# Neighbourhood attention: probabilities cut into half-precision parts before they are turned, and turned by DMA transposes

## The chip, the cores and the metric

The kernel runs on one core of a Trainium2 chip. Its time is the device time of one execution in microseconds (us), from the first instruction to the last, as a median over runs. The core has five engines with queues of their own: PE (TensorE, the matrix multiplier), DVE (VectorE), ACT (ScalarE), POOL (GpSimd) and SP (SyncE, which here only issues transfers). Each works through its instructions in a fixed order, and they meet through semaphores. Transfers are issued from a queue and carried by 16 DMA engines.

## The reference, cut to what matters

The program is two layers over 1024 latent tokens (a 16 by 64 grid) and 256 context tokens of width 1024. The change touches only the attention of the second layer. Each of 16 heads (64 wide) has every latent token attend to a window of keys around it and to all 256 context tokens:

```
def row_block(r):
    rs = jnp.clip(r - kh // 2, 0, rows - kh)
    ...
    s_loc = jnp.einsum("bcqhd,bicjhd->bhcqij", q_r, k_b).astype(jnp.float32) * scale + bias[None]
    s_loc = jnp.where(col_ok[:, :, None, :], s_loc, -jnp.inf)
    s_ctx = jnp.einsum("bcqhd,bjhd->bhcqj", q_r, kc).astype(jnp.float32) * scale
    s = jnp.concatenate([s_loc.reshape(B_, H, n_chunk, NA_QCOLS, n_loc), s_ctx], axis=-1)
    p = jax.nn.softmax(s, axis=-1).astype(v.dtype)
    ...
    o = (jnp.einsum("bhcqij,bicjhd->bcqhd", p_loc, v_b)
         + jnp.einsum("bhcqj,bjhd->bcqhd", p[..., n_loc:], vc))
```

## The kernel before

Everything is float32 by contract. Products are made from two parts per operand, a high and a low one, so that a product is three matrix multiplications (high by high, high by low, low by high).

The attention is cut into 64 **items**: 8 pairs of heads, two halves of the grid (8 rows each), two heads, two pairs of column chunks. An item holds two chunks of 128 queries (8 rows by 16 columns). For each chunk there are 384 local keys (12 rows by 32 columns) and 256 context keys, so an item has two local blocks of 128 by 384 probabilities and one context block of 128 by 512 for both chunks. `attn_item` (L1724) is a generator with three **stages**, and `attention` (L1698) steps it:

- **Scores** (stage 0): two bias tiles `g` are loaded (L1733; a DMA of 192 KB each on SP's queue, through the helper at L268; the pool behind `g` has four buffers, so two items' worth), and PE forms the context scores and two local score blocks in PSUM.
- **Softmax and turning** (stage 1): DVE takes the context maximum (L1749), adds bias and takes the local maximum in one instruction per chunk (L1752), and negates it (L1754). ACT writes the exponentials with their sums: the context ones into a tile `t` (L1755), the local ones over the bias tile `g` (L1757). Then each block is turned, since the values' product needs the keys on the partitions: PE transposes it in float32, 128 by 128 at a time, into PSUM (L1764, 3 + 4 + 3 of them per item), ACT casts the result to a float16 high part (L1767), and DVE subtracts that to give the float16 low part (L1768).
- **Weighted values** (stage 2): PE multiplies the turned parts with the float16 value parts (30 small products per item, 64 columns wide), and ACT scales the result by the reciprocal sum into `s` (L1794). After the fourth item of a half, `attn_out` (L1800) turns that on PE, splits it and writes it to DRAM (`d<-tk`, from POOL's queue).

Between the stages `attention` runs a filler, `prep`: the projections of the next pair of heads (`attn_prep`, matmuls into `pq`) and, once these are used up, the first part of the attention's output projection. Step k begins item k's scores one step ahead of its softmax, and its values one step behind its softmax. `attn_prep` also loads the value tiles (`t<-d`, 17 DMAs a pair on SP's queue) and moves halves of the query parts across partitions with DMAs on POOL's queue (`s<-s`).

The Python order is only a proposal: a scheduler with a timeline model sets the order in which each engine gets its instructions, and pools of buffers (`pg` for `g` with 4, `pt` for `t` with 6, `pk` for `tk` with 4, `p2` for `s` with 35) decide where an instruction must wait for a free buffer.

Of the kernel before, what the change touches and what calls it, by code (L numbers as in the profile page):

```python
# [12 lines left out]
F16 = mybir.dt.float16  # L13
# [3 lines left out]
MUL, ADD, SUB, MAX, MIN = ALU.mult, ALU.add, ALU.subtract, ALU.max, ALU.min  # L17

P = 128
# [181 lines left out]
class Builder:  # L201
# [1496 lines left out]
    def attention(self, u, fill):  # L1698
        self.prep = {}
        self.od = [[self.DR([P, LAT]) for _ in range(2)] for _ in range(8)]  # L1700
        self.banks = 6
        n = sum(self.attn_prep(0, u))
        prep = (x for pr in range(1, 9) for x in (self.attn_prep(pr, u) if pr < 8 else fill))
        load = (x for pr in range(8) for x in self.attn_load(pr))
        items, done = [], 0
        ahead = 1
        for k in range(64 + ahead):
            it = next(load, None)
            if it is not None:
                items.append(it)  # L1710
            for stage in range(3):
                i = k - ahead - stage
                if 0 <= i < 64:
                    next(items[i], None)
                while done < (k * 3 + stage + 5) * n / 24:
                    done += next(prep)
        for it in items[-2:]:
            for _ in it:
                pass
        self.banks = 8  # L1720
        for _ in prep:
            pass

    def attn_item(self, head, hd, hf, c0, qs, kk, kc, vt, osb, out):  # L1724

        nc, a = self.nc, self.a
        rlo = 4 * hf
        bias, loc = [], []
        pctx = self.PS()
        for i in (0, 1):  # L1730
            c = c0 + i
            b = self.G(F32, 384)
            self.ld(b, a["bias"][head, hf, c])  # L1733
            bias.append(b)
            q = [t[:, c * P:(c + 1) * P] for t in qs]
            for part in (0, 1):
                self.mm(pctx[:, i * 256:i * 256 + 256], q[part], kc, part == 0, part == 1)
        for i in (0, 1):
            c = c0 + i
            q = [t[:, c * P:(c + 1) * P] for t in qs]  # L1740
            ps = self.PS()
            for part in (0, 1):
                kv = kk.rearrange("p (r w) -> p r w", w=64)[:, rlo:rlo + 12, KSTART[c]:KSTART[c] + 32]
                self.mm(ps[:, :384], q[part], kv, part == 0, part == 1)
            loc.append(ps)
        yield
        st = self.pt.tile([P, 16], F32, tag="st", name=self.nm("st"))
        cm, mx, nm, s1, s2, rv = (st[:, 2 * i:2 * i + 2] for i in range(6))
        nc.vector.tensor_reduce(cm, pctx.rearrange("p (i k) -> p i k", i=2), axis=AX, op=MAX)  # L1749
        pc = self.T()  # L1750
        for i in (0, 1):
            nc.vector.tensor_tensor_reduce(bias[i], loc[i][:, :384], bias[i], 1.0, cm[:, i:i + 1], ADD, MAX,  # L1752
                                           mx[:, i:i + 1])
            nc.vector.tensor_scalar(nm[:, i:i + 1], mx[:, i:i + 1], -1.0, None, op0=MUL)  # L1754
            nc.scalar.activation(pc[:, i * 256:i * 256 + 256], pctx[:, i * 256:i * 256 + 256], AF.Exp,  # L1755
                                 bias=nm[:, i:i + 1], accum_out=s2[:, i:i + 1])
            nc.scalar.activation(bias[i], bias[i], AF.Exp, bias=nm[:, i:i + 1], accum_out=s1[:, i:i + 1])  # L1757
        nc.vector.tensor_tensor(s1, s1, s2, ADD)
        nc.vector.reciprocal(rv, s1)
        pts = [None] * 3  # L1760
        for k, src, n in ((1, bias[0], 3), (0, pc, 4), (2, bias[1], 3)):
            ps = self.PS()
            for j in range(n):
                nc.tensor.transpose(ps[:, j * P:(j + 1) * P], src[:, j * P:(j + 1) * P], self.ident)  # L1764
            t = self.S2(F16, 1024)
            w = n * P
            nc.scalar.copy(t[:, :w], ps[:, :w])  # L1767
            nc.vector.tensor_tensor(t[:, 512:512 + w], ps[:, :w], t[:, :w], SUB)  # L1768
            pts[k] = t
        yield  # L1770
        o = self.PS()
        if hf not in osb:
            osb[hf] = self.S2()
        for i in (0, 1):
            c = c0 + i
            ops = []
            for g in range(3):
                gg = hf + g
                v = vt[c][:, gg * P + hd * 64:gg * P + hd * 64 + 64]
                vl = vt[c][:, 512 + gg * P + hd * 64:512 + gg * P + hd * 64 + 64]  # L1780
                ops.append((pts[1 + i], g, v, vl))
            for j in range(2):
                v = vt[4][:, j * P + hd * 64:j * P + hd * 64 + 64]
                vl = vt[4][:, 256 + j * P + hd * 64:256 + j * P + hd * 64 + 64]
                ops.append((pts[0], 2 * i + j, v, vl))
            oo = o[:, i * 64:(i + 1) * 64]
            for n, (t, j, v, vl) in enumerate(ops):
                ph, pl = t[:, j * P:(j + 1) * P], t[:, 512 + j * P:512 + (j + 1) * P]
                self.mm(oo, ph, v, n == 0, False)
                self.mm(oo, ph, vl, False, False)  # L1790
                self.mm(oo, pl, v, False, n == 4)
        for i in (0, 1):
            c = c0 + i
            nc.scalar.activation(osb[hf][:, c * P + hd * 64:c * P + hd * 64 + 64], o[:, i * 64:(i + 1) * 64],  # L1794
                                 AF.Copy, scale=rv[:, i:i + 1])
        if out is not None:
            self.attn_out(out, hf, osb[hf])
        yield
# [412 lines left out]
```

## Time and profile before

| what | us |
|---|---|
| runs | 3013.22, 3014.71, 3016.25 (median 3014.71) |
| profiled execution, its time | 3012.68 |
| its span, first to last instruction | 3010.8 |
| attention, from the first local maximum (L1752) to the last low part (L1768) | 1812.7 to 2280.3 |
| the same as 64 items | 7.3 each |
| PE busy over the span | 2890.9 (96%) |
| DVE, ACT, POOL busy over the span | 2075.4, 1359.2, 479.1 |

The page gives busy time by engine and by group of instructions, and for the idle time before an instruction what ended it. A group is named by the line that issued it, the engine, the operation and "written tile <- read tiles". Most operations go through helpers, so L283 is any matmul, L268 any DMA from SP, L274 any DMA from POOL, L289 the low part of a split, L287 the high part. A busy PE is not PE at its peak: its spans overlap and include its pipeline, so that one instruction's span can be longer than the time it adds.

### The profile page before, as it was taken

Reading aid. Unit: us, or ns where it says so; the run is one execution under the profiler, and the core shown is the slowest. Engines: PE = TensorE matmul, PEld = TensorE weight load, DVE = VectorE, ACT = ScalarE, POOL = GpSimd, SP = SyncE. Lnnn points to the kernel's source line nnn. Section 1 sums busy time; section 2 is a strip of 40 time slices with the busy share of each in tenths; the row PEclk is TensorE's granted clock in tenths of the full one; section 3 lists DMA queues with packets and bytes.
Section 4 is the critical chain, followed back from the end, with each engine's and each line's share of the span. In section 5 each row is a group of like instructions: output and inputs, shape, how many; then the busy total and the mean of one; then the engine's idle time right before and its main releaser. Section 6 shows DMA issues by size and latency. Waiting matters only on the chain. (4 is left out here: it accounts for less than half of the span.)

```text
span 3010.8 us, 45798 instructions
## 1 busy us (share of the span) xinstructions
PE 2890.9 (96%) x16320; PEld 2414.9 (80%) x16320; DVE 2075.4 (69%) x3988; ACT 1359.2 (45%) x2545; POOL 479.1 (16%) x789
## 2 busy tenths in 40 slices
PE   7899999899999999999999999999899999999997
PEld 2678888888899788788888888878777788888886
DVE  5677786684677777876777437777767886755555
ACT  3453315453455333333455336777665533333432
POOL 2112013352110111212010000110111021202000
PEclk9999999999999999999999999999999999999999
DMA  7764445356555454658884334444555265525663
GB/s 279 249 222 169 166 166 176 113 185 233 187 182 201 175 179 179 215 189 318 313 297 155 126 128 124 125 135 130 169 189 195 95 246 203 189 102 189 221 192 125
DMA packets 263486, 559.30 MB, mean 186 GB/s; under 512 B 33878, under 2 KB 85784, under 8 KB 263258
## 3 DMA queue, kind: packets, MB, share of 16 engines
q1 hardware_dynamic: 204474, 371.79, 37.7%
q0 software_dynamic: 56480, 180.40, 16.7%
q10 hardware_dynamic: 2304, 4.20, 0.4%
q8 instruction: 128, 2.10, 0.3%
q14 instruction: 100, 0.82, 0.1%
HBM read 418.63 MB, written 119.80 MB: 179 GB/s over the span
## 5 line engine op out<-in xcount | busy, mean ns | idle before, releaser
L1283 PE MATMUL ps<-s,s 128*128 128x512 f32 x2028 | 503.6, 390 | 9.2 <-ACT g L1288 3.5
L1283 PEld LDWEIGHTS ps<-s,s 128*128 128x128 f32 x2028 | 379.6, 188 | 93.8 <-ACT g L1288 6.4
L283 PE MATMUL ps<-s,wh 128*128 128x256 f32 (+1 forms) x1780 | 397.1, 328 | 3.1 <-DVE s L720 2.0
L283 PEld LDWEIGHTS ps<-s,wh 128*128 128x128 f32 x1780 | 295.2, 189 | 38.2 <-ACT wh L287 2.5
L283 PE MATMUL pq<-s,wh 128*128 128x512 f32 (+1 forms) x972 | 296.1, 383 | 0.7 <-DVE s L2039 0.7
L287 ACT CAST wh<-ws 128x1024 fp32r<-128x1024 f32 (+1 forms) x139 | 142.4, 1025 | 338.7 <-PE ps L283 160.2
L1454 PE MATMUL ps<-s,s 128*128 128x512 f32 (+1 forms) x1000 | 258.0, 383 | 3.2 <-DVE s L289 3.1
L283 PE MATMUL ps<-s,wl 128*128 128x256 f32 (+1 forms) x890 | 258.7, 327 | 1.0 <-DVE wl L289 1.0
L289 DVE TENSOR_TENSOR wl<-ws,wh 128x1024 fp32r<-128x1024 f32 (+1 forms) x139 | 165.4, 1191 | 136.3 <-ACT wh L287 132.9
L287 ACT CAST s<-s 128x1024 fp32r<-128x1024 f32 (+2 forms) x184 | 168.5, 940 | 185.3 <-DMA s<-d 161.5
L283 PE MATMUL ps<-s,s 128*128 128x64 f16 (+3 forms) x2663 | 217.8, 234 | 25.8 <-DVE st L1752 11.8
L287 ACT CAST s<-t 128x512 fp32r<-128x512 f32 (+2 forms) x250 | 139.7, 579 | 182.7 <-DVE t L1262 77.3
L289 DVE TENSOR_TENSOR s<-s,s 128x1024 fp32r<-128x1024 f32 (+2 forms) x162 | 186.9, 1185 | 49.1 <-ACT s L287 48.7
L1454 PEld LDWEIGHTS ps<-s,s 128*128 128x128 f32 x1000 | 184.5, 188 | 41.4 <-DVE s L289 4.9
L283 PEld LDWEIGHTS pq<-s,wh 128*128 128x128 f32 x972 | 175.6, 190 | 33.8 <-DVE s L1667 1.2
L289 DVE TENSOR_TENSOR s<-t,s 128x512 fp32r<-128x512 f32 (+2 forms) x250 | 165.4, 676 | 50.9 <-ACT s L287 31.7
L1283 PE MATMUL ps<-s,wh 128*128 128x512 f32 x608 | 192.2, 393 | 0.0
L283 PE MATMUL ps<-s,mat 128*128 128x512 f32 x684 | 175.7, 402 | 5.2 <-ACT s L287 4.3
L283 PE MATMUL pq<-s,wl 128*128 128x512 f32 (+1 forms) x486 | 179.3, 379 | 0.0
L283 PEld LDWEIGHTS ps<-s,wl 128*128 128x128 f32 x890 | 164.1, 189 | 18.8 <-DVE wl L289 1.7
L283 PEld LDWEIGHTS ps<-s,mat 128*128 128x128 f32 x684 | 130.0, 192 | 39.9 <-ACT s L287 6.6
L1454 PE MATMUL ps<-s 128*128 128x512 f32 (+1 forms) x500 | 149.1, 385 | 0.0
(382 smaller groups left out, 5622.1 us busy)
## 6 DMA issues: line engine op xcount, KB each, us to landing
s<-d SPq DMA_DIRECT2D x282, 256.0 KB, 3.6
s<-in_down SPq DMA_DIRECT2D x150, 256.0 KB, 4.1
d<-s POOLq DMA_DIRECT2D x137, 256.0 KB, 3.3
d<-tk POOLq DMA_DIRECT2D x98, 256.0 KB, 3.4
s<-in_ada_w POOLq DMA_DIRECT2D x48, 512.0 KB, 4.6
g<-in_bias SPq DMA_DIRECT2D x128, 192.0 KB, 2.8
ws<-in_up SPq DMA_DIRECT2D x44, 512.0 KB, 3.3
d<-g POOLq DMA_DIRECT2D x87, 256.0 KB, 3.2
```

Of the source, the lines that this page charges most:

```text
L283: self.nc.tensor.matmul(o, l, r, start=st, stop=sp)
L287: self.last_hi = nc.scalar.copy(hi, src).ins
L289: self.last_lo = eng.tensor_tensor(lo, src, hi.bitcast(F32), SUB).ins
L1283: nc.tensor.matmul(ps, x[:, sl], y, start=first and j == 0 and x is wh and y is xh, stop=j == 3 and x is wl, skip_group_check=True)
L1454: m = nc.tensor.matmul(acc[j][:, c0:c1], x[:, sl], y[:, xs], start=first and k == 0, stop=last and k == 2, skip_group_check=True)
```

## The change

Each of the three blocks of an item is now cut into its float16 parts where it lies, queries on the partitions: high and low part side by side in one tile `x` of 128 by 2w (w is 384 or 512). ACT casts the two local blocks (into `tk`), DVE casts the context block (into `t`). DVE subtracts for the local blocks, POOL for the context block. Then one DMA transpose per block, on SP's queue, writes the turned parts to the tile that the values' product reads. PE's transposes and the PSUM tiles for them are gone. The biases are loaded from POOL's queue instead of SP's, and the weighted values of an item come a step later than before (two steps behind its softmax); the loop runs one step more.

```
-        for k in range(64 + ahead):
+        for k in range(65 + ahead):
...
-                i = k - ahead - stage
+                i = k - ahead - stage - (stage == 2)
...
-            self.ld(b, a["bias"][head, hf, c])
+            self.ldr(b, a["bias"][head, hf, c])
...
         for k, src, n in ((1, bias[0], 3), (0, pc, 4), (2, bias[1], 3)):
-            ps = self.PS()
-            for j in range(n):
-                nc.tensor.transpose(ps[:, j * P:(j + 1) * P], src[:, j * P:(j + 1) * P], self.ident)
+            w = n * P
+            x = self.T(F16, 1024) if k == 0 else self.TK(F16, 1024)
+            if k:
+                nc.scalar.copy(x[:, :w], src[:, :w])
+            else:
+                nc.vector.tensor_copy(x[:, :w], src[:, :w])
+            (nc.vector if k else nc.gpsimd).tensor_tensor(x[:, w:2 * w], src[:, :w], x[:, :w], SUB)
             t = self.S2(F16, 1024)
-            w = n * P
-            nc.scalar.copy(t[:, :w], ps[:, :w])
-            nc.vector.tensor_tensor(t[:, 512:512 + w], ps[:, :w], t[:, :w], SUB)
-            pts[k] = t
+            nc.sync.dma_start_transpose(t[:, :2 * w].rearrange("p (n c) -> p n c", c=P), x[:, :2 * w])
+            pts[k] = (t, w)
...
-            for n, (t, j, v, vl) in enumerate(ops):
-                ph, pl = t[:, j * P:(j + 1) * P], t[:, 512 + j * P:512 + (j + 1) * P]
+            for n, ((t, w), j, v, vl) in enumerate(ops):
+                ph, pl = t[:, j * P:(j + 1) * P], t[:, w + j * P:w + (j + 1) * P]
```

The scheduler then sets the orders anew. Three places show what moved. Numbers behind a name count tiles, so one name with one number is one tile.

SP's queue, late in the attention. Before, it holds the bias loads of item after item, with a value load among them (`t<-d` reads the values):

```order
L268 DMA t_23077<-d_16236 128x2x128
L268 DMA g_23019<-in_bias 128x384
L268 DMA g_23023<-in_bias 128x384
L268 DMA g_23122<-in_bias 128x384
L268 DMA g_23126<-in_bias 128x384
L268 DMA g_23245<-in_bias 128x384
```

With the change, at a like place (the `s<-d` rows load finished heads for the output projection):

```order
L1770 DMA_TRANSPOSE s_4758_22560<-tk_22557 128x6x128
L1770 DMA_TRANSPOSE s_4760_22565<-t_22562 128x8x128
L1770 DMA_TRANSPOSE s_4762_22570<-tk_22567 128x6x128
L268 DMA t_22680<-d_16236 128x2x128
L268 DMA s_4816_22849<-d_16979 128x512
L268 DMA s_4829_22926<-d_16980 128x512
L268 DMA s_4830_22928<-d_16981 128x512
L268 DMA s_4846_22980<-d_16982 128x512
L1770 DMA_TRANSPOSE s_4778_22665<-tk_22662 128x6x128
L1770 DMA_TRANSPOSE s_4780_22670<-t_22667 128x8x128
```

The biases have left SP, and three transposes an item stand between the loads of values, weights and finished heads, each behind the softmax of its item.

POOL's queue, a stretch within the attention. Before it held only transfers, here the query halves (`s<-s`) and finished heads (`d<-tk`):

```order
L274 DMA s_4499_21381<-s_4499_21381 64x512
L274 DMA s_4500_21382<-s_4500_21382 64x512
L274 DMA d_16984<-tk_21431 128x512
L274 DMA s_4501_21387<-s_4501_21387 64x512
L274 DMA d_16985<-tk_21432 128x512
```

Now:

```order
L274 DMA g_22531<-in_bias 128x384
L274 DMA d_16986<-tk_22506 128x512
L274 DMA d_16987<-tk_22507 128x512
L1768 TENSOR_TENSOR t_22562<-t_22546,t_22562 128x512
L274 DMA g_22629<-in_bias 128x384
L274 DMA g_22633<-in_bias 128x384
L1768 TENSOR_TENSOR t_22667<-t_22651,t_22667 128x512
L274 DMA g_22725<-in_bias 128x384
```

The context block's subtraction (L1768 on POOL) stands between the bias loads of later items, and the bias loads stand between the subtractions, so each can hold up the other.

DVE's queue. Before, the subtractions read PSUM and come right after the cast that precedes them, and the bias tile had been freed by PE:

```order
L1768 TENSOR_TENSOR s_4795_23156<-ps_23152,s_4795_23156 128x384
L1768 TENSOR_TENSOR s_4797_23164<-ps_23159,s_4797_23164 128x512
L1754 TENSOR_SCALAR st_23266<-st_23266 128x1
L1768 TENSOR_TENSOR s_4799_23171<-ps_23167,s_4799_23171 128x384
```

Now the subtraction is what frees a bias tile: `g_22412` and `g_22416` belong to one item, `g_22527` and `g_22531` to the next, and `g_22629`, the first bias of the third, needs one of their four buffers:

```order
L1768 TENSOR_TENSOR tk_22557<-g_22412,tk_22557 128x384
L1754 TENSOR_SCALAR st_22649<-st_22649 128x1
L1759 RECIPROCAL st_22544<-st_22544 128x2
L1768 TENSOR_TENSOR tk_22567<-g_22416,tk_22567 128x384
L1767 CAST t_22667<-t_22651 128x512
L1758 TENSOR_TENSOR st_22649<-st_22649 128x2
L1759 RECIPROCAL st_22649<-st_22649 128x2
L1768 TENSOR_TENSOR tk_22662<-g_22527,tk_22662 128x384
L1648 SCALAR_TENSOR_TENSOR s_4749_22520<-t_22515,c_16968,s_4749_22520 128x512
L1768 TENSOR_TENSOR tk_22672<-g_22531,tk_22672 128x384
L1752 ISA g_22629,st_22742<-ps_22637,g_22629,st_22742 128x384
```

Six rows lie between the subtraction that frees the second tile and the first use of a bias loaded into the pair.

## The prediction

> **What bounds the kernel now.** I read the stage's engine times first, since the change lies inside one stage, under the page's head.
>
> ```profile
> span 3010.8 us, 45798 instructions
> ```
>
> ```profile
> core 0: us, PE busy (x) PEld busy (x) DVE busy (x) ACT busy (x) POOL busy (x), PEclk, DMA share, GB/s
> 1815.00:2285.00 470.00, 438.66 (x4090) 378.59 (x4090) 343.91 (x910) 337.08 (x972) 60.13 (x113) 0.99 0.49 149
> ```
>
> The attention takes 470 us for 64 items, 7.3 us each. PE is busy for 439 of them and idle for 31; DVE and ACT have 126 and 133 us to spare, POOL does little, the DMA engines are used by half, the granted clock is 0.99. So PE sets the pace, but not alone: the waits of the engines in this stretch say more (who waited, for whom; us in total, times, longest).
>
> ```profile
> PE ps L283 <- DVE st L1752: 11.8, 11, 2.7
> PE ps L1764 <- DVE s L1768: 5.3, 9, 0.7
> SPq L268 <- PE ps L1764: 319.9, 111, 8.9
> DVE g L1752 <- DMA g<-in_bias: 5.6, 4, 2.6
> ```
>
> PE waits for DVE to free score banks and transpose banks. The third row is of SP's own queue: 111 times a load stood there until a transpose had freed a bias tile, 320 us in all. So biases are fetched as late as the four tiles allow, though the fourth row shows that DVE paid for it only 4 times. The chain of waits over this stretch has the three dearest cases:
>
> ```profile
> 1996.94 4.44 DMA g<-in_bias
> 2106.08 3.95 DMA g<-in_bias
> 2171.77 6.16 DMA g<-in_bias
> ```
>
> **What the change removes.** All 640 transposes leave PE, the casts of 64 x 3 blocks from PSUM leave ACT, as many subtractions leave DVE.
>
> ```profile
> 1815.00:2285.00 470.00, 88.07 (x640) 73.49 (x640) 0.99 0.49 149
> 2053.39 1.09 PE ps L1764 x10
> L1767 ACT CAST s<-ps 128x384 f16<-128x384 f32 x128 | 61.7, 482 | 36.3 <-PE ps L1764 34.9 <-PE ps L283 0.5
> L1767 ACT CAST s<-ps 128x512 f16<-128x512 f32 x64 | 37.6, 588 | 2.4 <-PE ps L283 2.0 <-PE ps L1764 0.2
> L1768 DVE TENSOR_TENSOR s<-ps,s 128x384 f16<-128x384 f32 x128 | 70.6, 552 | 16.1 <-ACT s L1767 14.3 <-DMA s<-s 1.0
> L1768 DVE TENSOR_TENSOR s<-ps,s 128x512 f16<-128x512 f32 x64 | 43.8, 684 | 8.1 <-ACT s L1767 7.7
> ```
>
> The first row is the transposes alone: 88 us of spans, which overlap. The chain has ten in a row in 1.09 us, and that is the time that they add: 64 x 1.09 = 70 us. Bounds are 70 and 88; I take 70, so PE keeps 439 - 70 = 369 us, 5.8 an item. The 10.9 us that PE idled before transposes go too, if no other wait inherits them; I count on none of it.
>
> ACT loses 2 x 0.482 + 0.588 = 1.55 us an item and DVE 2 x 0.552 + 0.684 = 1.79.
>
> **What it adds on the engines.** The new casts and subtractions read SBUF. The nearest rows:
>
> ```profile
> L287 ACT CAST s<-t 128x512 fp32r<-128x512 f32 x213 | 128.2, 620 | 161.4 <-DVE t L1262 77.3 <-POOL t L837 19.4 <-DMA d<-s 16.0
> L1376 DVE TENSOR_TENSOR g<-tk,g 128x512 f32<-128x512 f32 x65 | 44.8, 690 | 1.3 <-ACT g L1416 0.2
> L289 DVE TENSOR_TENSOR s<-s 128x256 fp32r<-128x256 f32 x22 | 8.5, 419 | 0.3 <-ACT s L287 0.3
> L837 POOL TENSOR_TENSOR t<-t,t 128x512 f32<-128x512 f32 x40 | 53.3, 1348 | 57.0 <-DVE t L836 56.0 <-ACT mat L335 0.4
> L783 POOL TENSOR_TENSOR s<-s,s 128x512 f32<-128x512 f32 x4 | 7.1, 1794 | 0.8 <-PE ps L283 0.8
> L274 POOL DMA_DIRECT2D s<-s x60 | 31.2, 521 | 163.9 <-ACT s L1679 101.6 <-DVE s L1768 16.1 <-ACT s L1794 10.6
> ```
>
> ACT: two casts of 384 columns, between 0.48 (the PSUM row above) and 0.62: 0.5 each, 1.0 an item, half a microsecond less than before. DVE: a 384-column subtraction lies midway between 0.69 and 0.42, 0.55 each; its one copy of 512 columns to half precision has no row; between half of 0.69 and all of it, I take 0.6 since the trace has no DVE copy that is faster. Sum 1.7 an item against 1.79: nothing gained or lost. POOL: one subtraction, 1.35 to 1.79 us, I take 1.35, its 40 instances being nearer in kind; and two bias issues of 0.52. POOL goes from 60 to 60 + 64 x (1.35 + 1.04) = 213 us, by the dearer row 241, of some 420: no bound by its sum.
>
> The Trainium skill (Advanced Engine Details and Errata, GPSIMD Details) says that POOL shares a read and a write interface with DVE and conflicts with DVE instructions that have two SBUF inputs; the new subtractions are such. By that rule DVE could lose POOL's 86 us of subtraction, an estimate: 344 + 86 = 430, some 10 us over the stage that I forecast. No run here shows such a loss.
>
> **The transposes by DMA.** The trace before has none. Each moves 128 x 768 or 128 x 1024 two-byte values, 192 or 256 KB, three an item, 0.66 MB; 41.9 MB in all. Rows for plain transfers of that size, and for SP's queue as a whole, over 1805 to 2285:
>
> ```profile
> q1 hardware_dynamic: 41696, 47.07, 33.3%
> g<-in_bias SPq DMA_DIRECT2D x124, 192.0 KB, 2.8
> s<-s POOLq DMA_DIRECT2D x60, 128.0 KB, 3.4
> d<-tk POOLq DMA_DIRECT2D x30, 256.0 KB, 3.4
> s<-d SPq DMA_DIRECT2D x24, 256.0 KB, 5.5
> ```
>
> Work on the 16 engines: q1 moved 47.07 MB in 33.3% of 480 us, 160 us, so 41.9 MB take 142 us at that rate. With 0.49 x 470 = 230 us of present traffic the sum is 372 us, under PE's 369 plus its idle time, though not by much. Below, nothing could make it cheaper than plain; above, half the plain rate gives 284 and a sum of 514. I take the plain rate, because the only transfer of the trace that also writes SBUF from SBUF (`s<-s`) lands in the same 3.4 us as the others.
>
> Latency: a step is to be some 6.5 us, and values now follow two steps behind the softmax, 13 us. The softmax and the cuts of an item use about 6 of these (five small DVE instructions, four exponentials, two casts, the subtractions); 7 are left for a landing of 2.8 to 5.5. Covered; if the landing were 10, PE, whose queue holds the value products in place, would stand still and everything queued behind them with it, the scores and projections.
>
> SP's queue keeps three instructions an item where two biases were; behind a transpose that waits for its softmax stand value and weight loads, which have an item or more of lead.
>
> **Where the stall goes.** Bias tiles were freed by PE's transposes and are now freed after a cast and a subtraction, and their loads stand in POOL's queue behind a subtraction of 1.35. The loop of one pair of tiles, two items long: landing 2.8, issue 0.52, two bias additions at 0.7, a negation 0.15, the exponentials, two casts 1.0, two subtractions 1.1, POOL's subtraction ahead 1.35. The rows for the remaining links:
>
> ```profile
> L1752 DVE CUSTOM_DVE_ANT_0 g<-ps,g,st 128x384 f32<-128x384 f32 x128 | 75.9, 614 | 46.2 <-PE ps L283 33.7 <-DMA g<-in_bias 5.6 <-DMA s<-d 3.7
> L1757 ACT ACTIVATE g<-g,st 128x384 f32<-128x384 f32 x128 | 79.2, 619 | 0.0
> L1755 ACT ACTIVATE t<-ps,st 128x256 f32<-128x256 f32 x128 | 61.2, 478 | 36.8 <-DVE st L1754 35.0 <-DVE st L1759 1.5
> L1755 ACT ACTIVATION_READ_ACCUMULATOR t<-ps,st 128x1 f32 x128 | 26.2, 204 | 0.0
> L1752 DVE DVE_READ_ACCUMULATOR2_ANT st<- 128x1 f32 x128 | 10.6, 83 | 0.0
> L1754 DVE TENSOR_SCALAR st<-st 128x1 f32<-128x1 f32 x128 | 17.4, 148 | 0.6
> L268 SPq DMA_DIRECT2D g<-in_bias x128: 327/328/1415, 1391.5 to 2269.8; - x128
> ```
>
> Exponentials: 2 x (0.48 + 0.62 + 2 x 0.2) = 3.0. Sum 11.3 us for two items, 5.7 an item; before, with PE's 0.33 for three transposes in place of casts and subtractions and SP's issue of 0.33, it was 8.0, 4.0 an item. So the loop moves from 3 us an item under the pace to just under the new one. Each time one of its links waits behind other work of its engine, a bias comes late. Bounds: nothing, or half of the added 3.3 us on each item, 64 x 1.65 = 106. I take 20 us, nearer the lower end, because DVE paid for late biases only 4 times so far.
>
> At the end the last item's values come one step later with the projection's filler partly used up; I put 4 us for the wait of the last heads, of a step of 6.5.
>
> **Sum.** 3012.68 - 70 + 20 + 4 = 2966.7 on the profiled execution, which lies 2.0 under the median of the runs: **2969 us**.
>
> **Rivals.**
>
> *Late biases eat it all.* The loop above, with waits at five or six of its links of 0.6 us each, comes to 14.6 us per two items, 7.3 an item: today's pace. For it: the 320 us on SP's queue, and POOL's queue, where a bias stands behind subtractions that wait for DVE. Against: only 4 late loads so far. Price: nothing gained or lost but the 4 us of the tail, about 3015, with some 20 us to either side.
>
> *The DMA engines become the bound (the slower side).* If a transposing transfer keeps the engines twice as long as a plain one, they need 514 us for the stage: 514 - 470 = +44, and 4 for the tail, 3063. It decides from 240 / 142 = 1.7 times the plain cost. For it: every value has to reach another partition, which no transfer of the trace does but `s<-s`, and that carries half the bytes in the same 3.4 us. Against: `s<-s` moves whole rows and is the nearest there is, and its landing is no worse than `d<-tk`'s.
>
> *One at a time.* If SP starts a transpose only when the one before has landed, three landings of 3.4 us are 10.2 an item, 653 us for the stage: +183, 3198. For it: one queue issues them all. Against: the bias loads are issued 0.33 us each, without waiting for a landing. The Trainium skill (VectorE: DVE Perf Modes, The three transpose paths) gives 1309 ns for a 128 by 128 block of half precision by DMA against 390 by TensorE; as an estimate, its 20 blocks an item one after another would be 26 us, 1676 for the stage and about 4220 in all. TensorE's blocks cost 109 ns here, so the trace doesn't bear out the other half of that row.
>
> **How the numbers follow.** Forecast 0.56; late biases 0.14 (of it 0.04 faster, 0.05 the same, 0.05 slower); DMA engines 0.20; one at a time 0.10. A measurement can't tell 0.2%, 6 us, from no change. Faster 0.56 + 0.04 = 0.60, the same 0.05, slower 0.05 + 0.20 + 0.10 = 0.35. The forecast's own range: with 88 - 70 = 18 us more from the transposes, the 11 of PE's waits and no late bias, 3014.7 - 88 - 11 + 4 = 2920, of which I use 2930; above, with the 106 us of late biases it ends in the first rival. The range for 8 in 10 reaches over that and the DMA engines' case, 3063 and a dozen more for its tail: **2930 to 3075**, with the one-at-a-time case and a little below left out.
>
> **What would show it.** PE's busy time in the attention near 369 and the stage near 420 us: the removal is right. No row of PE's waits ending in a DMA transpose: the latency is covered; such rows with tens of us mean a rival of the transfers, and the DMA share tells which: near 1 for the engines, below 0.8 for one at a time. DVE's wait for the bias loads near 20 us: the loop is sized right; over 60, the first rival. DVE's subtractions above 0.6 us each would mean contention with POOL. I am wrong if the attention lasts 470 us or longer.

## The result, and the profile after

The changed kernel takes **3088.93 us**, a median of 4 runs (3082.02 to 3094.14), against 3014.46 before (4 runs, 3013.22 to 3016.25): a ratio of 1.0249, 95% interval 1.0235 to 1.0263. It is slower, by 74 us; 2969 was forecast, in a range of 2930 to 3075. The mechanism is that of the rival named after the DMA engines, which was priced at 3063.

| us, in the profiled execution | before | after |
|---|---|---|
| span | 3010.8 | 3080.2 |
| from the start to the first bias addition (L1752) | 1812.7 | 1826.6 |
| first to last bias addition, called the attention from here on | 460.8 | 503.9 |
| from the last one to the end | 737.3 | 749.7 |

So 43 of the 69 us come from the attention, 14 from ahead of it and 12 from behind it. The engines' busy times over the attention in the changed kernel (columns as in the prediction):

```profile
core 0: us, PE busy (x) PEld busy (x) DVE busy (x) ACT busy (x) POOL busy (x), PEclk, DMA share, GB/s
1826.60:2330.50 503.90, 395.59 (x3302) 326.96 (x3301) 353.57 (x899) 305.38 (x889) 198.78 (x289) 0.88 1.04 211
```

PE lost its transposes, 396 us busy and not 430 over the same piece, and now idles for 108 us. The one figure at its limit is the DMA share: 1.04, where 0.48 stood before. (It can pass 1: in the two kernels of transfers below it is up to 1.02 where one queue is at work and 1.04 to 1.14 where two are.) The granted clock has gone from 0.99 to 0.88. What the engines waited for from 1815 to 2365 us, a little over both ends of the attention (who, for whom; us in total, times, longest):

```profile
PE ps L283 <- DMA s<-tk: 56.8, 22, 13.4
PE ps L283 <- DVE st L1752: 23.2, 20, 3.7
PE ps L283 <- DMA s<-t: 14.5, 9, 5.1
ACT tk L1765 <- DMA s<-tk: 60.6, 22, 8.9
DVE tk L1768 <- ACT tk L1765: 51.0, 26, 9.9
DVE g L1752 <- DMA g<-in_bias: 33.4, 26, 4.5
POOL g L274 <- DVE tk L1768: 103.2, 60, 10.8
```

Read from the top, these make one ring. PE waits at the value products for turned blocks, 71 us in all. ACT waits with the next cast because the four tiles `tk` come free only when a transpose has landed. DVE's low parts wait for that cast, POOL's bias loads for the low parts that free a bias tile, DVE's next softmax for the bias. Two of its links end in a transfer, the turned blocks and the biases. The queues' part of the 16 engines in the attention (packets, MB, share of the time), and the median time to landing:

```profile
DMA packets 201270, 106.21 MB, mean 211 GB/s; under 512 B 170572, under 2 KB 186175, under 8 KB 201215
q1 hardware_dynamic: 186911, 60.71, 68.4%
q0 software_dynamic: 14304, 44.84, 34.7%
...
g<-in_bias POOLq DMA_DIRECT2D x124, 192.0 KB, 4.7
...
s<-tk SPq DMA_TRANSPOSE x124, 5.4
...
s<-t SPq DMA_TRANSPOSE x62, 5.8
```

68.4% and 34.7% of 503.9 us are 345 and 175 us, together 520: all the time there is. Some 165 thousand of the packets under 512 bytes are new (5933 stood there before): 40.6 MB of transposes in pieces of about 250 bytes. The chain of waits has the late ones in line (start, us, what):

```profile
2219.15 8.96 DMA s<-tk
...
2230.67 14.18 DMA s<-tk
...
2270.53 9.58 DMA s<-tk
...
2338.05 13.97 DMA s<-tk
```

The last of these lies behind the last softmax: the values of the last items wait for it, and the filler is used up.

### The profile page after: what moved, and what is told of

Its sections match the earlier page's. It is cut to its first block, busy times and chain, and to the rows that moved or that the text cites. A ratio compares the mean times of both kernels' runs of the same rounds, so it can differ in the third digit from the quotient of the medians.

```text
span 3080.2 us, 45180 instructions
## 1 busy us (share of the span) xinstructions
PE 2865.4 (93%) x15680; PEld 2375.8 (77%) x15680; DVE 2093.7 (68%) x3988; ACT 1333.7 (43%) x2481; POOL 628.2 (20%) x981
## 5 line engine op out<-in xcount | busy, mean ns | idle before, releaser
L283 PE MATMUL ps<-s,s 128*128 128x64 f16 (+3 forms) x2663 | 240.7, 241 | 117.9 <-DMA s<-tk 56.8
L283 PE MATMUL pq<-s,wh 128*128 128x512 f32 (+1 forms) x972 | 313.4, 402 | 9.8 <-DVE s L1680 3.6
L283 PEld LDWEIGHTS pq<-s,wh 128*128 128x128 f32 x972 | 189.2, 205 | 44.6 <-DVE s L1680 4.9
L283 PE MATMUL pq<-s,wl 128*128 128x512 f32 (+1 forms) x486 | 187.8, 396 | 0.0
L283 PEld LDWEIGHTS ps<-s,s 128*128 128x128 f32 (+1 forms) x743 | 121.4, 202 | 52.6 <-DVE st L1752 13.9
```

Source lines behind the costliest of these rows:

```text
L283: self.nc.tensor.matmul(o, l, r, start=st, stop=sp)
```

## The experiments

**Is it turning, or moving the bytes at all? The latency, or the rate?** Three kernels vary the transfer alone. The first copies the same bytes and leaves the turning out, the second turns only the high parts and leaves the low ones out, the third gives every transfer a step more.

```
- nc.sync.dma_start_transpose(t[:, :2 * w].rearrange("p (n c) -> p n c", c=P), x[:, :2 * w])
+ nc.sync.dma_start(t[:, :2 * w], x[:, :2 * w])                                         (e1)
+ nc.sync.dma_start_transpose(t[:, :w].rearrange("p (n c) -> p n c", c=P), x[:, :w])    (e6)
- i = k - ahead - stage - (stage == 2)
+ i = k - ahead - stage - 2 * (stage == 2)                                              (e2)
```

> The changed kernel with each DMA transpose replaced by a plain SBUF to SBUF transfer of the same bytes on the same queue with the same waits (the probabilities are not turned, so this leaves the turning out). Theory A, a transposing transfer keeps the 16 DMA engines about twice as long as a plain one and they are full: the DMA share of the attention falls from about 1.05 to 0.9 or less, landings from 5.4 us to under 4, and the time to 2950 to 2990 us. Theory B, late biases through POOL's queue set the pace: the time stays above 3050. Theory C, the bytes themselves are too many whatever the kind: above 3050, with the share still near 1.

> The changed kernel with only the high halves transposed (96 and 128 KB instead of 192 and 256) and the high part used in place of the low one; the low parts are left out of the result. Theory A (DMA engines full by transposes): half of the transposes' time is gone, the share falls to about 0.8, the time to 2960 to 3000 us. Theory B (late biases): above 3050. Theory D, a fixed time per transpose on SP's queue, independent of its size: no gain, SP's row for a transpose stays at 1.26 and 1.52 us and the time above 3050.

> The changed kernel with the weighted values yet another step later. Theory A (full DMA engines, a limit of rate): the time stays at 3070 us or more, since a later consumer does not make the engines faster. Theory E, only the latency of the transposes is uncovered: PE's waits for transposes fall from about 71 us to under 20 and the time to 3020 or less.

Measured, one time each: 3007.7, 3009.25 and 3074.98 us, beside 3014.14 for the kernel before (8 runs, 3008.73 to 3022.69). The attention over its own piece, plain copies first, then half the transposes:

```profile
1832.30:2259.40 427.10, 370.34 (x3343) 309.64 (x3342) 359.85 (x897) 302.78 (x886) 199.05 (x290) 0.94 0.80 248
```

```profile
1822.00:2270.00 448.00, 382.50 (x3360) 319.31 (x3359) 364.12 (x900) 304.58 (x888) 199.95 (x290) 0.92 0.88 192
```

Unturned, the same bytes leave the engines at 0.80 and the attention at 427 us; with half the bytes turned it takes 448, with all of them 504. SP's issue of a transpose took 1.2 us (median) with half the bytes and 1.3 to 1.5 with all, and at 504 us there are 2.7 us for each of the 186 transposes, so it is not SP's issue that fills the stage. With a step more of slack the waits only move:

```profile
PE ps L283 <- DMA s<-tk: 6.8, 2, 5.8
ACT tk L1765 <- DMA s<-tk: 68.1, 23, 12.9
DVE g L1752 <- DMA g<-in_bias: 48.8, 37, 3.2
```

PE's wait for `s<-tk` falls from 57 to 7 us and the attention stays at 499.8. Here slack cured the late transfers, and not the engines that had too much to do. The totals of e1 and e6 are above what was expected: both lose time ahead of the attention (1832 and 1822 against 1812.7), on which more below. So even with the turning left out, the rest of the change was worth about 6 us (3007.7 against 3014.14) and not the 46 that were forecast.

**What a transpose costs by itself.** Two kernels leave out the whole computation. They hold transfers of 256 KB between SBUF tiles, 64 in a stretch with eight tiles to write to, and in some stretches bias loads of 192 KB on GpSimd's queue:

> Leaves out the whole computation (the output is zeros) and runs five stretches of 64 transfers each, one after the other: 256 KB copies from SBUF to SBUF on SP's queue; the same bytes by transposing DMA; 192 KB bias loads on GpSimd's queue; copies and bias loads together; transposes and bias loads together. Theory A (a transposing transfer keeps the 16 engines about twice as long as a plain one, whatever runs beside it): the copies take about 57 us of engine time (16.8 MB at q1's 47.07 MB per 160 us), the transposes 105 to 125 us with the DMA share at 0.9 or more, the bias loads about 43 us, transposes with bias loads about 150 to 170 us, the sum of the two. Rival B (SP's issue of 1.26 us each sets the rate): 64 transposes last 81 us with a share below 0.8, and 85 with the bias loads beside them. Rival C (transposes are only slow beside other traffic): alone 57 to 70 us, with bias loads well over the sum of the two.

> Leaves out the whole computation again (zeros are put out), five stretches of 64 transfers of 256 KB from SBUF to SBUF: copies in rows of 2 KB on SP; copies in pieces of 256 bytes on SP (the tile that is written has gaps); transposes on SP; pieces of 256 bytes with the 192 KB bias loads on GpSimd's queue; transposes with copies on GpSimd's queue. Copies alone ran at 380 GB/s and transposes alone at 190 with the DMA share at 1.0, and transposes with bias loads took 178 us where the two alone add up to about 127. Theory A (the price of a transpose is that of its 256-byte packets): the pieces run at 180 to 200 GB/s too, 85 to 95 us, and beside the bias loads they too take 160 us or more. Rival (the turning itself costs, or SP's issue of 1.3 us): the pieces run at 300 GB/s or more, 55 us or less, and beside the bias loads 100 or less; then the transposes' stretch still takes 88 us.

The stretches of the first in its order (copies; transposes; bias loads; copies with bias loads; transposes with bias loads):

```profile
core 0: us, DVE busy (x) POOL busy (x), PEclk, DMA share, GB/s
15.80:63.50 47.70, 3.61 (x33) 0.00 (x0) 1.00 0.95 352
64.00:152.00 88.00, 2.17 (x19) 0.00 (x0) 1.00 1.00 187
155.00:200.00 45.00, 4.69 (x55) 37.96 (x72) 1.00 0.86 298
203.00:275.00 72.00, 0.82 (x6) 28.32 (x53) 1.00 1.04 380
277.00:455.00 178.00, 3.79 (x37) 34.21 (x64) 1.00 1.08 165
```

And of the second (copies; pieces of 256 bytes; transposes; pieces with bias loads; transposes with copies on GpSimd's queue):

```profile
21.00:64.00 43.00, 2.05 (x19) 0.00 (x0) 1.00 0.99 369
68.00:143.00 75.00, 2.62 (x33) 0.00 (x0) 1.00 1.00 213
149.00:236.00 87.00, 2.30 (x15) 0.00 (x0) 1.00 1.01 188
240.00:347.00 107.00, 2.33 (x28) 34.29 (x64) 1.00 1.08 268
353.00:545.00 192.00, 3.18 (x23) 32.92 (x62) 1.00 1.14 172
```

Alone, with nothing beside it, a transpose keeps the engines 87 / 43 = 2.0 times as long as a copy. Most of that goes with the size of its pieces: a copy in pieces of 256 bytes takes 75 / 43 = 1.7 times (the 75 us lie between the 85 to 95 of the theory and the 55 of its rival). The second half of the theory fell. Beside bias loads on GpSimd's queue the pieces do no harm (107 us, where 75 and 45 add up to 120), nor do whole copies (72, where 43 and 45 add up to 88), but transposes do: 178 us where 88 and 45 add up to 133. Beside copies on GpSimd's queue they took 192, where 87 and 43 (the copies on SP's queue) add up to 130. The 178 hold two parts: up to 384 us the loads and 18 of the transposes are issued, 107 us for what takes some 67 apart (45 for the loads, 22 for the 4.17 MB turned by then), and from 384 the other transposes run alone at their old rate (192 GB/s). So the price is two things: a factor of 2 that transposes show with nothing beside them, and a further one where they meet traffic on GpSimd's queue. Why they slow each other stays open, and no run mixes transposes with a queue other than GpSimd's. In these stretches, copies and transposes had this median time to landing:

```profile
t<-x SPq DMA_DIRECT2D x64, 256.0 KB, 3.0
```

```profile
t<-x SPq DMA_TRANSPOSE x64, 3.4
```

3.0 against 3.4 us, with twice the time on the engines: the landing does not show the price.

**The other two parts of the change, and the kernel before as a control.**

```
- self.ldr(b, a["bias"][head, hf, c])        the changed kernel, biases back on SP (e3)
+ self.ld(b, a["bias"][head, hf, c])
- self.ld(b, a["bias"][head, hf, c])         the kernel before, biases on GpSimd (p1)
+ self.ldr(b, a["bias"][head, hf, c])
- for k in range(64 + ahead):                the kernel before, values an item later (p2)
-     i = k - ahead - stage
+ for k in range(65 + ahead):
+     i = k - ahead - stage - (stage == 2)
```

> The kernel before, unchanged, as a control for what the changed kernels lose outside the attention: in the profile of before GpSimd idles until 16.3 us ahead of its first mask and ScalarE's first square of x starts at 11.97 us; in all five profiles of changed kernels the mask is made at 3.4 us, the square starts at about 16.6, and the attention starts 6 to 20 us later. If that comes from the run and not from the kernel, the square may start at 16.6 here too and the attention at 1817 or later; if it comes from the change, the square starts at 12.0 and the attention's first addition of a bias at 1812.7 within 1.5 us. The attention itself lasts 459 to 463 us in either case, and the time is 3009 to 3023 us.

> The changed kernel with its bias loads back on SP's queue. Theory A (the DMA engines are full): the attention stays at 495 to 510 us and the time at 3075 to 3095, since the same bytes are moved; the DMA share stays over 0.93. Rival (late biases behind GpSimd's subtractions cost their own 20 us or more): the attention falls to 485 or less, the time to 3065 or less. Or the other way: bias loads now stand behind transposes of 1.26 us issue each on SP, which wait for the softmax; then VectorE's wait for biases goes from 33 us to 60 or more and the time above 3100.

> The kernel before with only its bias loads moved to GpSimd's queue. If the queue matters by itself (the prediction's loop), VectorE's wait for biases goes from 5.6 us to 15 or more and the time up by 8 to 20 us. Theory A: biases are late in the changed kernel because the engines that carry them are full; here they are half idle, the wait stays under 10 us, the attention at 461 within 4, the time at 3014 within 6.

> The kernel before with only the values an item later, transposes on PE. Nothing in before waits for the casts (PE waits at the value products for a cast are not among its rows), so the attention stays at 458 to 464 us and the time at 3010 to 3024; the rival that the later values cost by themselves (buffers of turned blocks held longer, the tail) would show as an attention of 466 or more or as 5 us or more after its last bias addition, 737.3 before.

c0: 3012.63 us, with the attention at 1812.7 and 460.6 long, as in the profile of before. (It is one run; p1, as fast as before, begins its attention 6.4 us later.) e3: 3090.25, one time and within the runs of the changed kernel, attention 508.9, DMA share 0.92 (a little under the 0.93 expected). p1: 3012.48 (10 runs, 3003.81 to 3021.15) against 3012.85, a ratio of 0.9990 (0.9975 to 1.0005). p2: 3020.1, one time, attention 467.2 and 739.5 behind it. That is over the 466 at which the later values were to cost something by themselves; 6 us of the attention at most, in a time that the runs of before nearly reach (3008.4 to 3019.45). So the bias queue costs nothing and the later values little beside the 74. DVE's wait for biases in p1 and in e3:

```profile
DVE g L1752 <- DMA g<-in_bias: 9.7, 11, 1.5
```

```profile
DVE g L1752 <- DMA g<-in_bias: 60.1, 33, 10.1
```

On GpSimd's queue with half-idle engines (a share of 0.48) VectorE waits 10 us for biases. Back on SP they stand behind transposes, and SP waits 62 us there for VectorE's low parts: VectorE's wait grows to 60 us, and the total doesn't show it. p1 also gives what the queues cost without the transposes:

```profile
q0 software_dynamic: 14558, 45.69, 32.6%
q1 hardware_dynamic: 21965, 20.41, 14.6%
```

And this is q1 in e1, with the same bytes unturned:

```profile
q1 hardware_dynamic: 48512, 60.18, 42.6%
```

Of 462 us, p1's share is 67 for q1; in the changed kernel it was 345, so the transposes took 277 us, where the same bytes unturned (42.6% of 427.1 us, 182) took 115. Half the bytes turned (e6, q1 at 45.9% of 448 us) took 138, half of 277: it goes by bytes. In the kernel the factor is 2.4: the 2.0 from above, and some 1.2 that fit the mixture. This second factor is no constant: with the biases on SP's queue, and 74 us of GpSimd's traffic in place of 175, the same working gives 242 us, a factor of 2.1 (e3, q1 at 77.4% of 508.9 us, of which 152 are what it carried before).

**Less on the engines.** First only the context block by DMA, the rest as before (e4). Then the same with the local blocks turned a step after their softmax, in a stage of their own (v1), and those stages with no DMA transpose at all (v2):

```
  for stage in range(4):                                        (v1, v2)
      i = k - ahead - stage
  ...
  e = self.TK(F32)                   exponentials beside the bias tile, not over it
  nc.scalar.activation(e[:, :384], bias[i], AF.Exp, ...)
  ...
  nc.sync.dma_start_transpose(t.rearrange("p (n c) -> p n c", c=P), x)     context (v1)
  yield
  ...                                local blocks on PE, as before
```

> Only the context block (256 KB an item) by DMA transpose, the two local blocks by PE as before, biases on SP's queue, values a step later. Theory A: 16.8 MB of transposes are 40% of the added engine time, so the DMA share stays under 0.85 and the landing is covered; PE saves 4 of 10 transposes, 28 us, less some waits: 2985 to 3005 us, a gain on the kernel before. Theory B does not apply (biases are freed by PE as before). Theory D or E: above 3014, with PE waiting for transposes.

> A version after the theory that the DMA engines must not be filled and PE must not wait for the softmax: only the context block is turned by DMA, the two local blocks on PE one step after their softmax (a stage of its own), values a step after that, exponentials of the local blocks written to tiles of their own so that a bias tile comes free at once; biases on SP. Theory A: 16.3 MB of transposes at 190 GB/s are 86 us of engine time on top of 0.48 x 462 = 222, a share near 0.7, so the engines don't bind; PE keeps about 411 us and the waits for ACT's exponentials of the first context-only version (19.7 us) go: attention 430 to 448 us, time 2990 to 3010 with the 5 to 12 us that changed kernels lose before and after it. Rival (ScalarE and VectorE's own loop of softmax and casts sets the pace at 7.2 us an item, whatever PE does): attention 458 or more, time 3015 or more.

> The same stages without any DMA transpose: all ten blocks of an item on PE, one step after the softmax. PE's work is that of the kernel before, 439 us in 470; only its waits of some 20 us can go. Attention 445 to 460 us, time 2998 to 3014. If the softmax loop of ScalarE and VectorE sets the pace, 458 or more and no gain; if the DMA transposes of v1 are worth anything, this is 10 us or more slower than v1.

e4: 3035.71 (5 runs), 1.0065 (1.0044 to 1.0085), 30 us over the top of what was expected. Attention 462.9, DMA share 0.69, transposes landing in 3.3 us: the engines no longer bind, and yet nothing is won, and PE now waits at the local blocks' transposes (L1775 there) for the softmax:

```profile
PE ps L1775 <- ACT g L1757: 19.7, 9, 7.4
```

v1: 3027.19 (4 runs), 1.0052 (1.0037 to 1.0067). Its attention took 446.0, 15 us less than before and as expected; the total wasn't, since 14 us are lost ahead of it and 13 behind. v2: 3021.22 (10 runs), 1.0025 (1.0013 to 1.0038), over the 3014 expected, attention 459.4: the stage by itself brings nothing, and the transposes of v1 are worth 13 us inside the attention. In the total v2 is 6 us shorter than v1, which loses more than that around it.

**What is lost around the attention.** Each of the seven profiles with the context's subtraction on GpSimd starts in another way than the eight without. The timeline of GpSimd and ScalarE in the changed kernel, and in x1, which has that subtraction on VectorE and turns the last two items on PE:

```profile
3.42 0.31 POOL masks.py:199 TENSOR_SCALAR_AFFINE_SELECT c<-c 128x128 f32<-128x128 f32 x1 [0.34 <-issue]
16.59 1.06 ACT L1857 ACTIVATE s<-s 128x1024 f32<-128x1024 f32 x1 [6.12 <-DMA s<-in_x_row]
```

```profile
16.47 0.28 POOL masks.py:199 TENSOR_SCALAR_AFFINE_SELECT c<-c 128x128 f32<-128x128 f32 x1 [13.37 <-issue]
13.18 1.06 ACT L1865 ACTIVATE s<-s 128x1024 f32<-128x1024 f32 x1 [4.31 <-DMA s<-in_x_row]
```

In the first, GpSimd does not stand still for 13 us ahead of its mask; the four large loads queued behind the mask then leave at 3.7 and not at 16.7, beside the rows of x, and ScalarE gets its first row 3.4 us later. That the loads delay the row is argued from this order alone. v3 is v1 with both edits, v4 has the context's cast on ScalarE besides.

```
- (nc.vector if k else nc.gpsimd).tensor_tensor(x[:, w:2 * w], src[:, :w], x[:, :w], SUB)
+ nc.vector.tensor_tensor(x[:, w:2 * w], src[:, :w], x[:, :w], SUB)
+ if head == 15 and hf == 1:         transposes on PE, as before
```

> The changed kernel with the context's subtraction on VectorE instead of GpSimd, and with the last two of the 64 items turned on PE. Theory (the subtraction on GpSimd moves the program's start; the last transposes, which landed in 14 us beside the loads of the next layer, set the tail): ScalarE's first square of x back at 12 to 13 us, first bias addition at 1812 to 1821, and 736 to 742 us behind the last one; the attention itself still 495 to 510, since the engines carry nearly the same bytes; time 3062 to 3078. If neither is the cause: square at 16.4 or later, 748 or more behind, time 3080 or more.

> The version with only the context block by DMA and the local blocks turned on PE in a stage of their own, now with the context's subtraction on VectorE and the last two items turned on PE altogether. The same theory: square at 12 to 13 us, attention from 1812 to 1821, lasting 446 to 455 (VectorE is 43 us busier, 385 of some 450), 736 to 742 behind it: 2996 to 3012 in all, at or under the kernel before. If VectorE has no room: attention 458 or more, 3012 or more.

> v3 with the context's cast to half precision on ScalarE, whose busy time is the lowest of the three: VectorE some 359 us busy, ScalarE some 335. If VectorE's load mattered in v3, the attention is 3 us or more shorter than there; if the chain from softmax to transpose does (ScalarE's cast then stands behind the next exponentials), no shorter. 2994 to 3012 us.

x1: 3057.63 (4 runs, 3055.32 to 3076.91), 1.0152 (1.0116 to 1.0188). First row at 13.18 us, attention from 1819.4 to 2322.7 (503.3, unchanged), 730.9 behind it against 749.7. The start is near what the theory had (12 to 13 us, and 1812 to 1821), the piece behind the attention is shorter than its 736 to 742, and the attention's loss of 43 us stands. Both edits are in x1, so which of them shortened the tail isn't shown. v3: **2999.48** (5 runs, 2994.23 to 3000.36), **0.9942 (0.9925 to 0.9960)**: faster than both kernels.

```profile
1813.20:2246.20 433.00, 401.30 (x3683) 343.54 (x3682) 354.44 (x959) 297.51 (x882) 55.44 (x103) 0.98 0.76 191
```

Attention 433.0, 28 us less than before, though VectorE has more to do than in v1; behind it 746.1 and not the 736 to 742 expected, so there the last transposes were not the cause. v4: 3004.51 (10 runs), 0.9962 (0.9948 to 0.9976), attention 444.4: relieving VectorE was no help. Why v3's attention is 13 us shorter than v1's no run shows; one effect of GpSimd's subtraction on VectorE can be read directly. The groups of the changed kernel in the attention (mean ns behind the bar), and the same subtraction in x1:

```profile
L1768 DVE TENSOR_TENSOR tk<-g,tk 128x384 f16<-128x384 f32 x128 | 86.2, 685 | 51.7 <-ACT tk L1765 51.0
...
L1768 POOL TENSOR_TENSOR t<-t,t 128x512 f16<-128x512 f32 x64 | 76.6, 1198 | 60.8 <-DVE st L1758 21.3 <-DVE st L1754 20.1 <-DVE t L1767 17.8
...
L1765 ACT CAST tk<-g 128x384 f16<-128x384 f32 x128 | 63.4, 511 | 66.5 <-DMA s<-tk 60.6 <-DMA d<-tk 5.1
L1767 DVE CAST t<-t 128x512 f16<-128x512 f32 x64 | 28.4, 444 | 7.8 <-ACT t L1755 6.8 <-issue 0.7
```

```profile
L1776 DVE TENSOR_TENSOR tk<-g,tk 128x384 f16<-128x384 f32 x124 | 67.3, 550 | 45.8 <-ACT tk L1773 45.2
```

VectorE's subtraction takes 685 ns in the mean beside GpSimd's and 550 without; its single instances go up to 1905 ns in the one and to 560 in the other. 128 x 0.135 = 17 us of VectorE's time are lost. The Trainium skill (SBUF — State Buffer, SBUF: two separate sides) has whichever of VectorE, with two inputs in SBUF, and GpSimd starts first hold their shared ports for its whole instruction, while the other waits. The trace agrees as to the waiting: each of the 11 instances over 650 ns that the timeline lists singly overlaps a GpSimd subtraction (median 1173 ns) and ends 0.41 to 0.43 us after it. It doesn't bear out that the first to start goes first: the two longest, 1.91 and 1.81 us, began 0.2 to 0.3 us ahead of GpSimd's and still ended behind it.

## Why the prediction was wrong, step by step

The forecast was off by 120 us: 93 in the attention (50 less forecast, 43 more measured), 14 ahead of it, 8 behind it, and 5 because the profiled execution lies 6.9 us under the median here and 2.0 before.

**What bounds the kernel now: right.** PE set the pace. With the bytes moved unturned (e1) PE is busy for 370 us, 369 forecast, and the attention is 34 us shorter, of the 50 forecast; PE's wait for the softmax (L1752) grew by about the rest, to 31.1 us there against 11.8 before. In the changed kernel itself PE was busy for 396 us, at a granted clock of 0.88: how much of its 43 us went through the lower clock, no run separates.

**The price of the transposes: the step that failed.** The prediction put 41.9 MB at the plain rate, 142 us, "because the only transfer of the trace that also writes SBUF from SBUF (`s<-s`) lands in the same 3.4 us as the others". The plain price was high by a fifth (115 us for 40.6 MB in e1, 138 at that rate). The turned one was 277, not known from any row of before. And the reason given could not have told: in m1 the two kinds land in 3.0 and 3.4 us, while 64 of them take 43 and 87 us of the engines (m2). With 277 in place of 142 and 230 of present traffic the prediction's own sum is 507, against 504 measured; that is no test of its own, since with the engines full the queues' times add up to about the stage whatever it lasts.

**The rival of the DMA engines: right in mechanism and in the stage** (+44 forecast, +43 measured). That the number fits so well is partly luck: its 284 us were 2 x 142, and the measured 277 are 2.4 x 115, so a plain price that was too high made up for a factor that was too low. Twice the 115 and the 230 would have been 460, under the 470 of the stage. Its test, a share near 1 with PE waiting for transposes, is what the page shows. What it lacked is 14 us ahead of the stage and 8 of the 12 behind.

**One at a time: excluded.** Transposes overlap, 1.4 us each at 3.4 us of landing in m1.

**Late biases: near in size, and only in part by the loop.** 20 us were put. DVE waited for biases 15.7 us in e1, which has the whole loop with the engines at 0.80, and 33.4 in the changed kernel (5.6 before, 9.7 in p1 with the queue alone), where bias loads land in 4.7 us in place of 2.8. What of these waits the stage paid, no run shows; in p1 it was nothing. (The upper bound was also misplaced: 106 us of late biases make 3055, which is over the first rival's 3015 with 20 to either side.)

**The engines' new work: right within 0.16 us an instruction.** Casts on ACT 0.51 us (0.5), VectorE's cast 0.44 (0.6), GpSimd's subtraction 1.2 (1.35), VectorE's 0.685 (0.55, and 0.55 without GpSimd). The prediction's sign for contention, over 0.6 us, has appeared; up to 86 us were given for it, and on these subtractions it came to 17, on an engine that waited for ACT anyway in this kernel.

**The tail: mis-sized, its cause open.** 4 us put, 12.4 measured. The prediction let the values of the last items wait a part of a step; in the changed kernel PE waits 13.8 us for transposes behind the last softmax, one of which took 14 us to land. x1, which turns the last items on PE, has no such wait and gave 18.8 us back. But the pieces behind the attention are 746.5 us in e1, which copies unturned, and 746.1 in v3, which turns the last items on PE, so these waits are not all of it.

**Ahead of the attention: not foreseen.** 13.9 us. ScalarE's first row comes 3.4 to 4.6 us later with the subtraction on GpSimd (x1, v3 and v4 have it early again); that the delay lasts to the attention isn't shown, and x1 begins it at 1819.4 all the same. Why GpSimd stands still for 13 us at the start of one program and not of the other stays open. The rest is not settled: p1, as fast as before, also begins its attention 6.4 us later in its profile, so part of it is the spread between runs.

## What to carry to other kernels

Price a transfer of a kind that the trace doesn't have by its bytes and the size of its pieces on the 16 engines, not by the landing of a single one; where the sum with the present traffic is near the stage's length, the doubled price is the case to plan for. To move work from the bounding engine, move as much as the taker has room for: one block of three by DMA, with the rest a step later, the subtraction off GpSimd and the last two items on PE, was worth 0.6%, all three cost 2.5%. And add up what an edit does ahead of and behind its stage; here that was over a third of the loss.

## What the runs showed that was not expected

- Transposes and transfers on GpSimd's queue slow each other: 178 and 192 us where the parts alone add up to 133 and 130; copies in 256-byte pieces beside the bias loads don't (107 of 120).
- Copies between SBUF tiles in pieces of 256 bytes ran at 213 GB/s, in rows of 2 KB at 369.
- One line more of work on GpSimd in the middle of a program went with another order of its first 17 us, in seven profiles of seven.
- The granted clock over the attention was 0.88 with PE idle for 108 us and 0.98 in v3; PE's busy time was 396 us and not the 370 of e1 at 0.94, about as the clocks (370 x 0.94 / 0.88 = 396).
